# Splitting the attention values in half-length buffers, at other steps around the turn of a head, with low parts made by a negated copy and an adding transfer

## The chip, the cores and the metric

One Trainium2 chip, one core. The metric is the time of one execution in device microseconds; lower is better. The times given are medians of several executions, and the profile is of one of them.

## The reference

One inference step of a decoder layer, for a prompt of 1024 positions and 8 sampled sequences of one position each, in float32. Only the first part of it, the differential attention of the prompt, is touched:

```python
def diff_attention(q, k, v, q_pos, k_pos, rel_bias, lam):
    ...
    def probs(qi, ki):
        s = jnp.einsum('bqhd,bkhd->bhqk', qi, ki).astype(f32) * scale + bias
        return jax.nn.softmax(jnp.where(mask, s, neg), axis=-1)

    attn = probs(q1, k1) - lam * probs(q2, k2)
    return jnp.einsum('bhqk,bkhd->bqhd', attn, v.astype(f32))

def reference(...):
    ...
        hp = rmsnorm(xp, norm_mix[l])
        qa, ka, va, qr, kr, vr, gr = project(hp, w_in[l])
        oa = diff_attention_prompt(qa, ka, va, rel_bias, lam)
        s_p, o_r = retention_prompt(...)
        xp = xp + merge_groups(oa, o_r, gr, subln_a[l], lam_init) @ w_out[l]
        xp = xp + mem_attend(rmsnorm(xp, norm_mem_q[l]), mk_p, mv_p, w_mq[l], w_mo[l])
        xp = xp + sq_relu_mlp(rmsnorm(xp, norm_mlp[l]), w_up[l], w_down[l])
    ... the same for the 8 sampled sequences, with a paged cache of 256 positions
```

There are 4 attention heads with values of width 128; `attn` is causal, so a block of 128 queries meets only the blocks of 128 keys up to its own.

## The kernel before, in words

**Exact products from fast ones.** The matrix engine works on `float32r`, a shorter float. Each operand is split in a high part (a copy that rounds to `float32r`) and a low part (the operand less its high part), and a product is three matmuls: high by high, high by low, low by high.

**The attention of the prompt** goes head by head. A head has ten items `(pr, kg)`: query pair `pr` (256 queries, 0 to 3) by key pair `kg` (256 keys, 0 to `pr`), in the order (0,0), (1,0), (1,1), (2,0), (2,1), (2,2), (3,0), (3,1), (3,2), (3,3). The loop `for g in range(-4, 40)` has one step per item; `h` is the head and `x` the item's number, 0 to 9, and `g` from -4 to -1 is a run-up (`h` = -1, `x` = 6 to 9). One step

- turns the probabilities of the next item (`turn`, `trA`): 3 or 4 transposes on TensorE, a rounding copy `ah` on ScalarE (L1034), the low part `al` on VectorE (L1035); for the item on the diagonal GpSimd clears a quarter of both (L1033);
- computes scores of later query blocks (`scores`, the list `SCORES`; steps 6 to 9 those of the next head): matmuls `sp` in one of 3 banks of PSUM, the masked minimum `mn` and the result `e` on VectorE (L1001), an exponential on ScalarE (L1007), and, after the second of the two maps, the weighted difference on VectorE (L1014 to L1016);
- weighs the values with the item (`weigh`, `av`): for each of two key blocks the three matmuls by `VH` and `VL`; an item with key pair `kg` reads the key blocks `2 * kg` and `2 * kg + 1`. After the last key pair of a query pair ScalarE copies the sum (L1053);
- fills the rest with matmuls of the next heads' query and key projection (`filler`, `qkp`), and in head 3 with the sampled sequences' decode (`dsc`).

**The values.** `fetch_values(h + 1)`, at step `x == VALUES_AT` (6), has SyncE's queue bring the next head's values from HBM into `vraw`, 512 KB, in a buffer of a ring of three (`raw`) that the weights, the broadcast row factors `rbh` and the decode's gathered keys `ck` share. `load_values(h)`, at `x == 0`, makes `VH` and `VL`, each one buffer of 1024 columns: for each half a copy on ScalarE (L975) and a subtraction on GpSimd, in one case on VectorE (L977). Key blocks 0 to 3 (`kg` 0 and 1) lie in the first half, blocks 4 to 7 (`kg` 2 and 3) in the second. So the first half is last read at step 7 of a head, and the second is first read at step 5 and last at step 9.

**What sets the order.** Every engine takes its instructions in one order, and so does each DMA queue (SyncE's and GpSimd's). Matmuls of this part keep the order of the program (`pin`). On the other engines the framework orders the instructions itself when the kernel is built, from their place in the program and its own estimates of when they can start; `tc.issue_after` puts some behind a named instruction. So an instruction can stand earlier than its step: the decode's gathers are written at steps 21 to 26 and are issued by GpSimd from 341.80 us on, in head 1.

Beside these, `load_part` (L949 to L958) prepares the next head's keys and queries, with transfers on GpSimd's queue (L950, L952), `norm_out` (L1119) scales the head before by `rbh`, and `operand_steps` (L1255) loads the output projection's operands, 2064 KB each, on GpSimd's queue.

Of the kernel before, what the change touches and what calls it, by code (L numbers as in the profile page):

```python
# [10 lines left out]
F32 = mybir.dt.float32  # L11
F32R = mybir.dt.float32r
I32 = mybir.dt.int32
AF = mybir.ActivationFunctionType
ALU = mybir.AluOpType
# [4 lines left out]
P = 128  # L20
D = 1024
NT = 1024
# [26 lines left out]
def decoder_step(ctx: ExitStack, tc: tile.TileContext, i: dict, o: dict):  # L49
    nc = tc.nc  # L50
# [47 lines left out]
    half = G.tile([P, 1], F32, tag="half", name="half")  # L98
# [86 lines left out]
    V = v_front.enter_context(pool("v"))  # L185
# [95 lines left out]
    with pool("s") as A:  # L281
# [64 lines left out]
        for t in range(9):  # L346
# [13 lines left out]
            if t in (1, 3, 5):  # L360
                k = t // 2 + 1
# [24 lines left out]
    with pool("a") as A:  # L386
# [56 lines left out]
        with behind("Activation", "DVE"):  # L443
# [3 lines left out]
            for k in range(4):  # L447
                src = t2f[k // 2][:, k % 2, :]
# [189 lines left out]
        A = r_front.enter_context(pool("r", side="right"))  # L638
# [245 lines left out]
    with pool("b") as A:  # L884
# [13 lines left out]
        def head_units(h):  # L898
            uqk[h] = [unit(U_QK + 2 * h + x) for x in range(2)]
# [61 lines left out]
        vraws = {}  # L961

        def fetch_values(h):
            vraw = vraws[h] = G.tile([P, 1024], F32, tag="raw", name=f"vraw_{h}", bufs=3)
            nc.sync.dma_start(
                vraw[:, :NT].rearrange("p (t v) -> p t v", t=8),
                o["v_p"][:, h * P : h * P + P].rearrange("(t p) v -> p t v", p=P),
            )

        def load_values(h):  # L970
            VH = A.tile([P, NT], F32R, tag="VH", name=f"VH_{h}")
            VL = A.tile([P, NT], F32R, tag="VL", name=f"VL_{h}")
            vraw = vraws[h]
            for cs in (slice(0, 512), slice(512, NT)):
                nc.scalar.copy(VH[:, cs], vraw[:, cs])  # L975
                eng = nc.vector if h == 3 and cs.start == 0 else nc.gpsimd
                eng.tensor_sub(VL[:, cs], vraw[:, cs], VH[:, cs].bitcast(F32))  # L977
            vals[h] = VH, VL
            oraws[h] = A.tile([P, NT], F32, tag="oraw", name=f"oraw_{h}", bufs=2)

        def scores(h, q, m):
            KA, KB, Q, M = stacks[h]
# [54 lines left out]

        def weigh(h, pr, kg):
            ah, al = trs.pop((h, pr, kg))
            VH, VL = vals[h]  # L1040
            nk = 2 * pr + 2
            if kg == 0:
                avs[h, pr] = PS.tile([P, 512], F32, tag="av", name=f"av_{h}_{pr}", bufs=1)
            av = avs[h, pr]
            for kk in range(2):
                k = 2 * kg + kk
                at_ = (1 - kk if kg == pr else kk) * 256
                ks, xs = slice(k * P, k * P + P), slice(at_, at_ + 256)
                mm(av[:, :256], VH[:, ks], ah[:, xs], k == 0, False)
                mm(av[:, :256], VH[:, ks], al[:, xs], False, False)  # L1050
                mm(av[:, :256], VL[:, ks], ah[:, xs], False, k == nk - 1)
            if k == nk - 1:
                nc.scalar.copy(oraws[h][:, pr * 256 : pr * 256 + 256], av[:, :256])  # L1053
# [275 lines left out]
        for g in range(-4, 40):  # L1329
            h, x = divmod(g, 10)  # L1330
            todo = []
            if g >= 0:
                if x == 0:
                    load_values(h)
                    if h < 2:
                        head_units(h + 2)
            if h < 3:
                if h >= 0 and x == EARLY_AT[0]:
                    load_stacks(h + 1)
                    until(h + 1, 1, 1)  # L1340
                    early = load_part(h + 1, EARLY)
                for y in (0, 1, 2, 3):
                    if h >= 0 and x == EARLY_AT[y]:
                        if y == 2:
                            until(h + 1, 1, 0)
                        next(early)
                if x == LATE_AT[0]:
                    until(h + 1, 2, 1)
                    late = load_part(h + 1, LATE)
                for y in (0, 1, 2, 3):  # L1350
                    if x == LATE_AT[y]:
                        if y == 2:
                            until(h + 1, 2, 0)
                        next(late)
            if x == VALUES_AT and h < 3:
                fetch_values(h + 1)
            if g in DECODE_AT:
                next(decode)
            if 0 <= g + 1 < 40:
                todo.append(lambda: turn(*items[g + 1]))  # L1360
            for q, m in SCORES.get(x, ()):
                hh = h + (x >= 5)
                if hh < 4:
                    todo.append(lambda q=q, m=m, hh=hh: scores(hh, q, m))
            if g >= 0:
                todo.insert(2, lambda: weigh(*items[g]))
            if h > 0:
                at_ = NORM_AT[h == 3]
                if x == at_[0]:
                    todo.append(lambda: sqs.append(norm_sums(h - 1)))  # L1370
                if x == at_[1]:
                    todo.append(lambda: sqs.append(norm_factors(h - 1, sqs.pop())))
                if x == at_[2]:
                    todo.append(lambda: sqs.append(norm_send(h - 1, sqs.pop())))
                if x == at_[3]:
                    todo.append(lambda: norm_row(h - 1, sqs.pop()))
                if x == at_[4]:
                    with tc.issue_after(seen["DVE"]):
                        norm_out(h - 1)
            dec = (3, 2, 0) in done  # L1380
            n = DFILL[g - 28] if dec else FILL - (g > 17)
            for y, f in enumerate(todo):
                f()
                for _ in range(shares(y + 1, n, len(todo), dec) - shares(y, n, len(todo), dec)):

                    if dec or (3, 2, 0) not in done:
                        next(filler, None)
            for _ in range(OPERAND_AT.count(g)):
                next(par)
            if g in OUT_AT:  # L1390
                for _ in range(OUT_AT[g]):
                    next(ahead, None)
            if g == LOADS_AT:

                for x, nm in enumerate(("KA0", "KA1", "KB0", "KB1")):
                    raw = A.tile([P, NT], F32R, tag=nm, name=f"raw_o{x}").bitcast(F32)
                    nc.sync.dma_start(raw, i["wall"][U_OUT + x])
                    raws_out.append(raw)
                onesb.append(A.tile([P, NT], F32, tag="M", name="onesb")[:, :P])
                nc.gpsimd.memset(onesb[0], 1.0)  # L1400
            if g in UNITS_AT:
                x = len(us_out)
                with tc.issue_after(seen["ACT"]), tc.issue_after(seen["E"]):
                    us_out.append(unit(U_OUT + x, raw=raws_out[x]))
# [3 lines left out]
        while len(us_out) < 4:  # L1408
            x = len(us_out)
# [1028 lines left out]
}  # L2438
EARLY_AT, LATE_AT = (3, 4, 4, 5), (7, 7, 8, 8)
NORM_AT = (2, 3, 4, 5, 8), (2, 5, 6, 8, 9)  # L2440
VALUES_AT = 6
DECODE_AT = (21, 22, 25, 26)
OPERAND_AT = (30, 30, 30, 33, 33, 34)
LOADS_AT, UNITS_AT = 32, (34, 35, 37, 38)
# [182 lines left out]
```

## Time and profile before

| | |
|---|---|
| median of 3 runs | 1493.73 us (1493.14 to 1497.79) |
| the profiled execution's span, first to last instruction | 1492.5 us |
| TensorE matmuls busy | 1474.0 us, 99% |
| VectorE, ScalarE, GpSimd busy | 1102.5, 678.4, 325.4 us |
| granted TensorE clock | 0.998 |
| the attention's value matmuls (`av`) | 271.6 to 442.5 us of the span |

The profiled execution's own time is its span and the little that lies around it; the median is 1.2 us above the span. In a row of a timeline stand the start and the duration in us, the engine, the line, the operation, what it writes and reads, and in brackets how long the engine had been idle before and what ended that. PE is TensorE, ACT ScalarE, DVE VectorE, POOL GpSimd, SPq the queue of SyncE. Each engine's row in the table is a busy time: what it is worth to shorten one depends on who waits for it.

### The profile page before, as it was taken

The numbers are of one execution on the slowest core, as the hardware profiler recorded it, in microseconds if no ns is written. First come the engines' busy times: TensorE is split into PE (matmuls) and PEld (weight loads), VectorE is DVE, ScalarE is ACT, GpSimd is POOL, SyncE is SP. The second block draws the span as 40 slices with busy tenths as digits, with TensorE's granted clock in tenths as the row PEclk, the third lists the DMA queues.
The fourth block names the chain that finished last, engine by engine and source line by source line (L and its number), as shares of the span: only waits on it lengthen the run. The fifth ranks groups of instructions, "written<-read, shape, count | busy, mean of one in ns | idle before, by whom it ended". The sixth has DMA issues, their size and how long they took to land.

```text
span 1492.5 us, 27826 instructions
## 1 busy us (share of the span) xinstructions
PE 1474.0 (99%) x10893; PEld 1402.5 (94%) x10893; DVE 1102.5 (74%) x2279; ACT 678.4 (45%) x1326; POOL 325.4 (22%) x346
## 2 busy tenths in 40 slices
PE   9999999998999999999999999999999999999997
PEld 7899779998769999989999999999999999999997
DVE  7656636987877734567786978888888889787875
ACT  7534435665652432147535634334344444343454
POOL 0035323114414321104132000000001311020380
PEclk9999999999999999999999999999999999999999
DMA  8155737214857157483592443344436674536273
GB/s 292 61 186 168 201 71 181 80 34 123 232 181 279 49 191 193 132 238 103 165 321 72 128 149 137 141 156 157 142 141 210 237 265 142 172 99 191 81 129 114
DMA packets 125229, 236.67 MB, mean 159 GB/s; under 512 B 13744, under 2 KB 76517, under 8 KB 124970
## 3 DMA queue, kind: packets, MB, share of 16 engines
q1 hardware_dynamic: 89056, 170.50, 36.5%
q0 software_dynamic: 24912, 44.80, 10.9%
q10 hardware_dynamic: 11130, 19.60, 3.5%
q8 instruction: 85, 1.39, 0.4%
q14 instruction: 46, 0.38, 0.1%
HBM read 170.24 MB, written 57.52 MB: 153 GB/s over the span
## 4 chain that ended last, share of the span: by engine, by line
PE 90%; DVE 5%; ACT 2%; issue 1%; DMA 1%; ACTq 0%; POOL 0%; DVEq 0%; SPq 0%
PE dn L2309 21%; PE Z L2143 9%; PE qkp L75 7%; PE pr_o L75 6%; PE mq L75 6%; PE pr_m L75 6%; PE X L2143 6%; PE Y L2143 6%; PE grp L75 3%; PE sp L75 2%; PE av L75 2%; PE mv L75 2%; PE mk L75 1%; PE mpv L75 1%; PE vap_z L522 1%
## 5 line engine op out<-in xcount | busy, mean ns | idle before, releaser
L2309 PE MATMUL dn<-UH,wd 128*128 128x258 f32 x1792 | 324.6, 283 | 0.0
L2309 PEld LDWEIGHTS dn<-UH,wd 128*128 128x128 f32 x1792 | 277.5, 189 | 0.7 <-ACT c L2410 0.2
L2309 PE MATMUL dn<-UL,wd 128*128 128x258 f32 x896 | 252.8, 282 | 0.0
L2309 PEld LDWEIGHTS dn<-UL,wd 128*128 128x128 f32 x896 | 169.0, 189 | 0.0
L2413 DVE TENSOR_TENSOR c<-c,dn 128x258 f32<-128x258 f32 x216 | 88.9, 418 | 38.5 <-PE dn L2309 36.1
L2169 ACT ACTIVATE hq<-r 128x258 f32<-128x258 f32 x128 | 53.7, 421 | 118.3 <-DVE r L2168 118.3
L2143 PE MATMUL Z<-T_h,wu 128*128 128x258 f32 x512 | 98.2, 284 | 0.0
L2143 PE MATMUL X<-UH,wu 128*128 128x258 f32 x512 | 97.4, 282 | 0.0
L2287 ACT CAST wd<-raw_d 128x512 fp32r<-128x512 f32 x96 | 58.8, 620 | 79.0 <-PE dn L2309 74.6
L1953 ACT CAST wu<-raw_up 128x512 fp32r<-128x512 f32 x96 | 59.1, 617 | 59.9 <-PE Z L2143 50.0
L2280 ACT CAST UH<-raw_h 128x1032 fp32r<-128x1032 f32 x56 | 58.7, 1056 | 53.5 <-PE dn L2309 27.7
L2143 PEld LDWEIGHTS X<-UH,wu 128*128 128x128 f32 x512 | 81.3, 188 | 0.2 <-ACT p L2194 0.2
L2143 PEld LDWEIGHTS Z<-T_h,wu 128*128 128x128 f32 x512 | 81.3, 189 | 0.0
L2180 POOL DMA_DIRECT2D HT<-ht x32 | 17.2, 538 | 292.3 <-DVE ht L2179 291.8
L2281 DVE TENSOR_TENSOR UL<-raw_h,UH 128x1032 fp32r<-128x1032 f32 x56 | 73.6, 1315 | 8.6 <-ACT UH L2280 8.6
L2288 DVE TENSOR_TENSOR wd<-raw_d,wd 128x512 fp32r<-128x512 f32 x96 | 72.2, 759 | 10.0 <-ACT wd L2287 9.9
L2143 PE MATMUL Z<-T_l,wu 128*128 128x258 f32 x256 | 72.3, 282 | 0.0
L2143 PE MATMUL X<-UL,wu 128*128 128x258 f32 x256 | 72.3, 282 | 0.0
L128 ACT CAST wh_u<-raw_u 128x1024 fp32r<-128x1024 f32 x43 | 44.6, 1047 | 54.3 <-PE mq L75 31.1
L1954 DVE TENSOR_TENSOR wu<-raw_up,wu 128x512 fp32r<-128x512 f32 x96 | 64.7, 687 | 3.5 <-ACT wu L1953 3.5
L2301 POOL TENSOR_TENSOR raw_d<-raw_d,raw_d 128x512 f32<-128x512 f32 x16 | 22.1, 1383 | 193.8 <-DVE raw_d L2297 172.9
L129 DVE TENSOR_TENSOR wl_u<-raw_u,wh_u 128x1024 fp32r<-128x1024 f32 x39 | 49.4, 1273 | 18.8 <-ACT wh_u L128 18.6
(597 smaller groups left out, 4732.8 us busy)
## 6 DMA issues: line engine op xcount, KB each, us to landing
raw_u<-in_wall SPq DMA_DIRECT2D x49, 512.0 KB
HT<-ht POOLq DMA_DIRECT2D x32, 516.0 KB
raw_h<-HT SPq DMA_DIRECT2D x32, 516.0 KB
raw_up<-in_wall SPq DMA_DIRECT2D x32, 512.0 KB
raw_d<-in_wall SPq DMA_DIRECT2D x32, 512.0 KB
HQ<-hq ACTq DMA_DIRECT2D x32, 387.0 KB
raw_h<-HQ SPq DMA_DIRECT2D x24, 516.0 KB
cmk<-in_cmk SPq DMA_DIRECT2D x16, 512.0 KB
```

The costliest lines, as they stand in the source:

```text
L75: pinned(nc.tensor.matmul(out, l, r, start=start, stop=stop))
L129: (lo_engine or nc.vector).tensor_sub(wl[:, :n], raw[:, :n], wh[:, :n].bitcast(F32))
L1953: nc.scalar.copy(w[:, :512], src)
L1954: nc.vector.tensor_sub(w[:, 512:], src, w[:, :512].bitcast(F32))
L2143: pinned(nc.tensor.matmul(ps, l, r[:, k, :], start=first and k == 0 and x == 0, stop=k == 3 and x == 2, skip_group_check=True))
L2169: nc.scalar.activation(h[:, PLACE[quad], :], r, AF.Square)
L2280: nc.scalar.copy(h, rv)
L2281: nc.vector.tensor_sub(l, rv, h.bitcast(F32))
L2287: nc.scalar.copy(w[:, :512], src)
L2288: nc.vector.tensor_sub(w[:, 512:], src, w[:, :512].bitcast(F32))
L2309: pinned(nc.tensor.matmul(ps, l, r[:, k, cq], start=first and k == 0 and x == 0, stop=k == 3 and x == 2, skip_group_check=True))
L2413: nc.vector.tensor_add(y, y, ps)
```

## The change

The values of a head get four buffers of 512 columns, `VH0`, `VL0`, `VH1`, `VL1`, in the place of two of 1024. The first half of the next head is split at step 8 of the head before it (two steps after the fetch), the second half at step 2 of its own head. The low part is no longer a subtraction: ScalarE writes the negated high part into it, and a transfer on GpSimd's queue adds the raw values to it. `weigh` reads the half that its key pair lies in. The tile that collects a head's result (`oraws`) is named at the first `weigh` in the place of `load_values`.

```diff
-        def load_values(h):
-            VH = A.tile([P, NT], F32R, tag="VH", name=f"VH_{h}")
-            VL = A.tile([P, NT], F32R, tag="VL", name=f"VL_{h}")
-            vraw = vraws[h]
-            for cs in (slice(0, 512), slice(512, NT)):
-                nc.scalar.copy(VH[:, cs], vraw[:, cs])
-                eng = nc.vector if h == 3 and cs.start == 0 else nc.gpsimd
-                eng.tensor_sub(VL[:, cs], vraw[:, cs], VH[:, cs].bitcast(F32))
-            vals[h] = VH, VL
-            oraws[h] = A.tile([P, NT], F32, tag="oraw", name=f"oraw_{h}", bufs=2)
+        def load_values(h, half):
+            vh, vl = (A.tile([P, 512], F32R, tag=f"V{x}{half}", name=f"V{x}{half}_{h}") for x in "HL")
+            src = vraws[h][:, 512 * half : 512 * half + 512]
+            nc.scalar.copy(vh, src)
+            nc.scalar.activation(vl, vh.bitcast(F32), AF.Copy, scale=-1.0)
+            nc.gpsimd.dma_start(vl, src, accum_op=ALU.add)
+            vals[h, half] = vh, vl
...
         def weigh(h, pr, kg):
             ah, al = trs.pop((h, pr, kg))
-            VH, VL = vals[h]
+            VH, VL = vals[h, kg // 2]
             nk = 2 * pr + 2
+            if (pr, kg) == (0, 0):
+                oraws[h] = A.tile([P, NT], F32, tag="oraw", name=f"oraw_{h}", bufs=2)
...
-                ks, xs = slice(k * P, k * P + P), slice(at_, at_ + 256)
+                ks, xs = slice(k % 4 * P, k % 4 * P + P), slice(at_, at_ + 256)
...
-                if x == 0:
-                    load_values(h)
-                    if h < 2:
-                        head_units(h + 2)
+                if x == 0 and h < 2:
+                    head_units(h + 2)
+                if x == VALUES_AT[2]:
+                    load_values(h, 1)
...
-            if x == VALUES_AT and h < 3:
+            if x == VALUES_AT[0] and h < 3:
                 fetch_values(h + 1)
+            if x == VALUES_AT[1] and h < 3:
+                load_values(h + 1, 0)
...
-VALUES_AT = 6
+VALUES_AT = 6, 8, 2
```

## The prediction, made before the change was run

> **What bounds the kernel now.** I read the page's head and its chain first, then the matrix engine's own waits and busy time in the attention part (235 to 445 us of the span), then the instruction timeline at the three turns of a head.
>
> ```profile
> span 1492.5 us, 27826 instructions
> PE 1474.0 (99%) x10893; PEld 1402.5 (94%) x10893; DVE 1102.5 (74%) x2279; ACT 678.4 (45%) x1326; POOL 325.4 (22%) x346
> ...
> PE 90%; DVE 5%; ACT 2%; issue 1%; DMA 1%; ACTq 0%; POOL 0%; DVEq 0%; SPq 0%
> ```
>
> TensorE is the bound: 1492.5 - 1474.0 = 18.5 us of it are idle in the whole span, and that is all that a change which touches no matmul can win. The waits of TensorE in the attention part, then its idle moments at the turns 1 to 2 and 2 to 3:
>
> ```profile
> PE sp L75 <- DVE mn L1001: 3.9, 4, 1.6
> PE trA L78 <- DVE e L1016: 2.6, 3, 2.0
> PE hrT L78 <- DVE c L1068: 0.3, 1, 0.3
> ...
> 352.12 0.41 PE L75 MATMUL sp<-KA,Q 128*128 128x320 f32 x1 [0.64 <-DVE mn L1001]
> 354.28 0.42 PE L75 MATMUL sp<-KA,Q 128*128 128x320 f32 x1 [1.60 <-DVE mn L1001]
> 359.87 0.55 PE L78 MATMUL trA<-ident,e 128*128 128x128 f32 x3 [2.03 <-DVE e L1016]
> 399.24 0.41 PE L75 MATMUL sp<-KA,Q 128*128 128x320 f32 x1 [0.82 <-DVE mn L1001]
> ```
>
> So 3.9 + 2.6 + 0.3 = 6.8 us are idle there (the columns of the first three lines: total, times, longest), all put down to VectorE, none to the values: no row says that a matmul waits for VH or VL. 0.64 + 1.60 + 2.03 = 4.3 us lie at the turn from head 1 to 2. In the stretch of the turn 0 to 1 TensorE is never idle, though the same reload is done there (columns: stretch, its length, busy time of TensorE's matmuls and weight loads, VectorE, ScalarE, GpSimd, then the granted clock, the DMA engines' share and GB/s):
>
> ```profile
> 300.00:310.00 10.00, 10.00 (x70) 9.79 (x69) 9.61 (x32) 6.32 (x20) 0.77 (x4) 1.00 0.00 0
> ```
>
> What the reload does to VectorE at the turn 1 to 2 is seen here:
>
> ```profile
> 355.25 0.21 DVE L1015 SCALAR_TENSOR_TENSOR mn<-mn,nlam,sm 128x1 f32<-128x1 f32 x1
> 356.76 2.50 POOL L977 TENSOR_TENSOR VL<-vraw,VH 128x512 fp32r<-128x512 f32 x2 [2.95 <-ACT VH L975]
> 356.84 1.22 DVE L1015 SCALAR_TENSOR_TENSOR mn<-mn,nlam,sm 128x1 f32<-128x1 f32 x1
> 358.45 1.37 DVE L1016 SCALAR_TENSOR_TENSOR e<-e,mn,e 128x512 f32<-128x512 f32 x1
> 403.50 0.75 DVE L1016 SCALAR_TENSOR_TENSOR e<-e,mn,e 128x512 f32<-128x512 f32 x1
> ```
>
> While the two subtractions run on GpSimd (356.76 to 359.26), one VectorE instruction takes 1.22 instead of 0.21 us, and one takes 1.37 instead of 0.75. The second ends at 359.82, and the transposes that wait for it start at 359.87.
>
> **The change, part by part.**
>
> *Low parts no longer subtracted.* These are the instructions that go, and the nearest row for what comes:
>
> ```profile
> L975 ACT CAST VH<-vraw x8: 615/622/625, 244.8 to 403.0; 128x512 fp32r<-128x512 f32 x8
> L977 POOL TENSOR_TENSOR VL<-vraw,VH x7: 1254/1287/1640, 245.5 to 403.7; 128x512 fp32r<-128x512 f32 x7
> L977 DVE TENSOR_TENSOR VL<-vraw,VH x1: 693/693/693, 402.9 to 402.9; 128x512 fp32r<-128x512 f32 x1
> 1424.48 17.95 POOL L2417 DMA_DIRECT2D c<-c  x20
> ```
>
> GpSimd loses 7 x 1.29 = 9 us and gains 8 issues of an adding transfer. The adding transfers at the end of the kernel take 17.95 / 20 = 0.90 us of it each: 7 us. Neither is on TensorE's path. What is, is the collision above: without it the two VectorE instructions end (1.22 - 0.21) + (1.37 - 0.75) = 1.6 us earlier. I take -1.5 us, since the 2.03 us wait bounds it at -2.0 and about half a microsecond of it then remains: late next is the same VectorE row, by its own queue. The other end is 0, if an issue of a transfer holds VectorE as a subtraction does. The one subtraction on VectorE, 0.69 us at 402.9, comes after the wait at 399.24 and I take 0 for it: the decode's matmuls, which fill head 3, cover it; without that cover it would be worth 0.69.
>
> *ScalarE's negated copies.* 8 x 0.62 = 5.0 us more (the row of VH; the copy of VL has that shape). In the window of 215 us ScalarE is busy 124.87, so it has 90 us of idle time, and the nearest gaps are these:
>
> ```profile
> 305.64 0.62 ACT L1007 ACTIVATE e<-e,mn 128x384 f32<-128x384 f32 x1 [2.10 <-DVE mn L1001]
> 350.53 0.48 ACT L1034 CAST ah<-trA 128x384 fp32r<-128x384 f32 x1 [2.38 <-PE sp L75]
> 394.18 0.51 ACT L1007 ACTIVATE e<-e,mn 128x256 f32<-128x256 f32 x1 [1.37 <-DVE e L1016]
> ...
> sum 215.00, PE 208.00 PEld 184.22 DVE 171.05 ACT 124.87 POOL 63.37; mean PE 11.56 PEld 10.23 DVE 9.50 ACT 6.94 POOL 3.52
> ```
>
> A pair of copies is 1.24 us, and each of the three gaps holds one. I count 0; 5.0 us is the ceiling if no gap were met. The second half, at step 2, waits for nothing (its buffer is free from the last matmul of the head before) and the gaps there are about 1 us: 0 as well.
>
> *Half buffers, filled from step 8 on.* The wait of the first copy for the last matmul of the old head goes; since no matmul waited for VH, that is worth 0. New is what the copies can wait for: the fetch of the raw values, still issued at step 6.
>
> ```profile
> 240.73 0.38 SPq L965 DMA_DIRECT2D vraw<-out_v_p  x1
> 340.89 0.49 SPq L965 DMA_DIRECT2D vraw<-out_v_p  x1
> 388.50 0.70 SPq L965 DMA_DIRECT2D vraw<-out_v_p  x1
> ...
> 244.76 1.14 ACT L975 CAST VH<-vraw 128x512 fp32r<-128x512 f32 x2 [1.83 <-DMA vraw<-out_v_p]
> ...
> 343.49 0.28 PE L75 MATMUL av<-ah,VH 128*128 128x256 f32 x1
> 392.24 0.28 PE L75 MATMUL av<-ah,VH 128*128 128x256 f32 x1
> ...
> 345.00:350.00 5.00, 5.00 (x34) 4.86 (x33) 3.79 (x12) 2.25 (x7) 3.92 (x7) 1.00 1.13 317
> 390.00:395.00 5.00, 5.00 (x39) 4.95 (x38) 3.34 (x15) 2.52 (x9) 4.16 (x7) 1.00 1.09 236
> ```
>
> The first fetch had landed 4.0 us after its issue, when the copy started that had waited 1.83 us for it. By that pace the fetches of heads 2 and 3 land at 344.9 and 392.5, just as the step 7 matmuls (343.49 and 392.24, the last readers of the half) are done. But the DMA engines are full there (shares 1.13 and 1.09), with the broadcast of a row, as large as the fetch and just ahead of it on SyncE's queue, and the decode gathers in the same stretch: twice 512 KB at half of the two rows' mean, 277 GB/s, is 7.5 us, so my estimate is 348.4 and 396. A ScalarE that stands at the copy holds up the exponentials queued behind it; VectorE waits for those, TensorE for VectorE. The floor is 0 (the gap before 350.53 takes it); the ceiling is 4 us at each turn (348.4 - 344.4, 396 - 393, and a pair of copies). As the order of ScalarE's queue is the framework's, I cannot read it; I take 0.5 us for both, near the floor, because the gap of 2.38 us stands just where the estimate falls.
>
> *The adding transfer's landing.* It must be there for the third matmul of the new head:
>
> ```profile
> 161.23 0.85 POOL L675 DMA_DIRECT2D OPH<-rh  x1 [1.06 <-ACT rh L672]
> 171.13 0.59 ACT L672 CAST rh<-trR 128x512 fp32r<-128x512 f32 x1 [3.66 <-DMA OPH<-rh]
> ...
> 362.13 0.28 PE L75 MATMUL av<-ah,VL 128*128 128x256 f32 x1
> 394.23 0.87 POOL L1255 DMA_DIRECT2D UL<-OPL  x1
> 407.60 0.27 PE L75 MATMUL av<-ah,VL 128*128 128x256 f32 x1
> ```
>
> The nearest transfer of 256 KB from GpSimd's queue, on full DMA engines, is known to be done 171.13 - 161.23 = 9.9 us after its issue. With copies done at 349.6 and 397.3 and that latency, VL lands at 359.5 and 407.2, before 362.13 - 1.5 = 360.6 and at 407.6: nothing, with no margin at the second. So 0 is taken, and 3 us is the other end, when GpSimd's in-order queue (the eight gathers, or the 2064 KB load at 394.23) is in front. The Trainium skill, "DMA: Bandwidth & Descriptors", section "Anatomy of one DMA — SWDGE (gpsimd) path", gives about 2.0 us fixed plus the bytes over 436 GB/s, by which an estimate for 256 KB is 2.6 us; the landing would then have 7 us to spare and this rival would be dead. The row of this trace does not agree, since it shows up to 9.9 us under load, and I go by the row.
>
> The buffer of the raw values is freed one half later. The next user of the last one is a pair of decode gathers:
>
> ```profile
> 409.19 1.00 POOL L859 DMA_INDIRECT ck<-in_cache_kT,idk  x1 [0.51 <-POOL al L1033]
> 427.58 1.07 PE L75 MATMUL dsc<-ck,qblkd 128*64 128x512 f32 x2
> ```
>
> 18 us lie between their issue and their matmul, and step 2 of head 3 is two steps of 4.5 us behind its step 0 (407.60 - 362.13 for ten), so it costs 0; if they land late, what is late next is that matmul, 1 us at most.
>
> **Sum:** -1.5 + 0 + 0 + 0.5 + 0 = -1.0 us against the profiled execution's span of 1492.5, thus 1491.5. The median of the runs shown, 1493.73, is 1.2 above that span: 1492.7 us. The difference from no change that a measurement of this kernel can tell is 0.3%, 4.5 us (1489.2 to 1498.2): I forecast no change.
>
> **Rivals.**
>
> *Slower: ScalarE stands at the fetch.* Place: the queue of ScalarE at steps 7 and 8 of heads 1 and 2. If the copies stand ahead of the exponentials there (394.18 above; the one of that shape at head 1 starts at 345.83, below), ScalarE waits from about 344 to 348 and from 393 to 396 or later.
>
> ```profile
> 345.83 0.51 ACT L1007 ACTIVATE e<-e,mn 128x256 f32<-128x256 f32 x1
> ```
>
> Price: 2 to 3 us on TensorE at each turn where part of a gap covers it, 4 where none does. Without the 0.5 us of the sum the forecast is 1492.2; one turn gives 1492.2 + 2.5 = 1494.7, both at their ceiling 1492.2 + 8 = 1500.2. It decides when the fetch lands more than 2.4 us after the copy's place in the queue; slower by 0.3% takes 6 us of it. For it: the rows of full DMA engines and the one copy that has already waited 1.83 us. Against: the gap of 2.38 us.
>
> *Cancelled: the transfer lands late.* TensorE then waits at the first value matmul for VL, 3 us at the turns 1 to 2 and 2 to 3 together: 1492.2 + 3 = 1495.2. For it the 9.9 us, against it the pace of the first fetch, 512 KB in 4.0 us.
>
> *Faster: VectorE's other waits go too.* The waits of 0.64, 1.60 and 0.82 us come from VectorE working off the low part of the last turned block ahead of the masks of (2,1) and (3,0). With ScalarE's order at step 8 new, these may swap as they stand at the turn 0 to 1, where TensorE has no wait. With the 2.03 that is 5.1 us: 1493.73 - 5.1 = 1488.6; the floor is all 6.8 us, 1486.9. Against it: no part of the change touches these instructions.
>
> **How the numbers follow.** The small gain (1490.5 to 1494.5) has 0.52; ScalarE at the fetch 0.28, of which 0.15 lies beyond 1498.2; the late landing 0.08; the faster rival 0.12. So faster 0.12, same 0.52 + 0.13 + 0.08 = 0.73, slower 0.15. The range for 8 in 10 runs from 1488.6, which leaves out half of the faster case (0.06), to 1499.0, which leaves out the worst of the first rival (0.11).
>
> **What would show it.** No GpSimd subtraction and no VectorE row of 1.2 us for a 128x1 at the turn 1 to 2; the wait of 2.03 us down to about 0.5; eight issues of about 0.9 us on GpSimd; ScalarE's first copies at steps 8 with no wait on the fetch. Wrong would be the forecast if ScalarE's waits on the fetch sum to over 3 us, if a value matmul waits for a DMA, or if TensorE's idle time in the attention part is under 3 or over 10 us.

## The result, and the profile after

The change made the kernel slower: 1503.04 us (median; 1501.62 to 1503.74) beside 1494.24 us of the kernel before on the same chip, a ratio of 1.0052, interval 1.0041 to 1.0062. Measured a second time, with other kernels beside it, the ratio was 1.0039 (1.0025 to 1.0053). The forecast was no change, with 1499.0 us as the upper end of its range.

The head of the page of the changed kernel, whose profiled execution took 1501.62 us:

```profile
span 1499.8 us, 27839 instructions
PE 1478.1 (99%) x10893; PEld 1405.3 (94%) x10893; DVE 1099.9 (73%) x2278; ACT 682.3 (45%) x1334; POOL 318.6 (21%) x347
```

The span grew by 7.3 us. TensorE is idle for 21.7 us instead of 18.5, and it is also busy for 4.1 us more, with the same 10893 matmuls. So part of the loss is a slower TensorE, not a waiting one.

To place the 7.3 us, I took from each trace the first score matmul (line 75, `sp`) and the first value matmul (`av<-ah,VH`) of each head; in the kernel before these stand at 255.31, then 271.56, 313.29, 361.90 and 407.25, and the last `av<-ah,VH` at 442.28. The distances between the starts of these matmuls, in us, for all kernels that were run:

| kernel | first score to head 0 | head 0 to 1 | 1 to 2 | 2 to 3 | 3 to last value matmul | ratio to before |
|---|---|---|---|---|---|---|
| before | 16.25 | 41.73 | 48.61 | 45.35 | 35.03 | 1 |
| before, second profile | 16.24 | 41.73 | 48.13 | 45.40 | 35.04 | 1 |
| changed | 18.56 | 41.73 | 49.02 | 49.90 | 35.04 | 1.0052 |
| changed, second profile | 19.74 | 41.69 | 49.22 | 50.81 | 35.04 | 1.0039 |
| changed, fetch at step 4 | 17.53 | 41.73 | 43.87 | 45.05 | 35.54 | 1.0017 |
| the same, second profile | 17.21 | 41.72 | 45.39 | 45.05 | 35.57 | 0.9996 |
| changed, head 0 subtracted | 16.24 | 41.73 | 46.50 | 50.45 | 35.03 | 1.0055 |
| both of these edits | 16.53 | 41.73 | 45.36 | 45.08 | 35.40 | **0.9977** |
| changed, copy behind (2,0) | 19.25 | 41.71 | 46.94 | 45.81 | 36.40 | 1.0008 |
| changed, copies written at the turn | 18.37 | 41.73 | 49.52 | 49.88 | 35.03 | 1.0040 |
| half buffers, subtraction | 16.24 | 42.78 | 49.08 | 49.42 | 35.04 | 1.0070 |
| the same, fetch at step 4 | 16.24 | 42.78 | 47.95 | 46.93 | 35.06 | 0.9990 |
| before, new low parts | 18.89 | 41.71 | 45.11 | 47.23 | 46.13 | 1.0096 |
| before, fetch at step 4 | 16.26 | 41.73 | 47.92 | 45.38 | 35.03 | 1.0000 |

Before against changed: 2.3 us are lost ahead of the first value matmul, 0.4 at the turn 1 to 2, 4.55 at the turn 2 to 3. That is 7.3 us, as much as the span grew. What lies ahead of the first score matmul is 0.6 us shorter and what lies behind the last value matmul 0.6 us longer, which cancels.

Each ratio compares a kernel with the kernel before on the same chip, but the chips differ. On the one where the first runs of "fetch at step 4", "head 0 subtracted", "half buffers, subtraction" and "before, new low parts" were made, the kernel before took 1490.64 us at a granted clock of 0.998 in most executions; on two others it took 1494.92 and 1495.62 us at 0.996. The one changed kernel that was run on both sorts, with the fetch at step 4, has 1.0017 on the first and 0.9996 on another. So ratios from different chips can differ by 0.2%; why the chips differ is not shown.

**The turns.** Timelines of the changed kernel: the fetch on SyncE's queue, ScalarE's first copy of the half, then what VectorE and TensorE wait for; first at the turn 1 to 2, then at 2 to 3 (start, length, engine and line; in brackets the idle time ahead of it and what ended it).

```profile
341.27 1.18 SPq L965 DMA_DIRECT2D vraw<-out_v_p  x1
351.08 0.62 ACT L973 CAST VH<-vraw 128x512 fp32r<-128x512 f32 x1 [5.31 <-PE av L75]
352.08 0.50 ACT L1004 ACTIVATE e<-e,mn 128x256 f32<-128x256 f32 x1
352.21 0.50 DVE L958 TENSOR_TENSOR Q<-qraw,Q 64x336 fp32r<-64x336 f32 x1 [4.01 <-ACT Q L957]
355.01 0.44 PE L78 MATMUL trA<-ident,e 128*128 128x128 f32 x2 [2.48 <-issue]
356.55 0.42 PE L75 MATMUL sp<-KA,Q 128*128 128x320 f32 x1 [0.63 <-DVE mn L998]
...
390.70 0.70 SPq L965 DMA_DIRECT2D vraw<-out_v_p  x1
398.92 0.62 ACT L973 CAST VH<-vraw 128x512 fp32r<-128x512 f32 x1 [3.92 <-PE sp L75]
399.45 0.50 ACT L1004 ACTIVATE e<-e,mn 128x256 f32<-128x256 f32 x1
402.35 0.69 PE L78 MATMUL trA<-ident,e 128*128 128x128 f32 x2 [3.39 <-DVE e L1013]
```

ScalarE stands still for 5.31 and 3.92 us ahead of the copy. The profile names a matmul as releaser, but the last `av` of the old half had ended at about 345.9, five microseconds earlier: the copy waited for the fetch, which was there 9.8 us after its issue (8.2 us at the other turn). Behind the copy in ScalarE's queue stands the exponential of block (1,1), 128x256; it starts at 352.08, while in the kernel before it started at 345.83 (that head began 1.75 us earlier there). VectorE waits for ScalarE, TensorE for VectorE.

The clock shows the second half of the loss (columns: stretch, its length, TensorE's busy time and matmuls, granted clock, DMA share, GB/s):

```profile
352.00:356.00 4.00, 1.44 (x9) 1.00 0.85 300
356.00:360.00 4.00, 3.40 (x14) 0.66 0.72 197
360.00:364.00 4.00, 4.00 (x26) 0.92 0.27 47
...
398.00:402.00 4.00, 0.96 (x5) 0.95 1.14 333
402.00:406.00 4.00, 3.54 (x8) 0.50 1.17 407
406.00:410.00 4.00, 4.00 (x12) 0.69 1.06 343
410.00:414.00 4.00, 4.00 (x18) 1.00 1.12 422
```

After the idle time the granted clock is at half for a while. (1 - 0.66) x 4 + (1 - 0.92) x 4 = 1.7 us of full-speed work are lost at the first turn, up to 0.2 + 2.0 + 1.24 = 3.4 at the second.

**The gain that was forecast.** At the turn 1 to 2 the pair of VectorE instructions that was stretched to 1.22 and 1.37 us beside GpSimd's subtractions now reads:

```profile
359.72 0.21 DVE L1012 SCALAR_TENSOR_TENSOR mn<-mn,nlam,sm 128x1 f32<-128x1 f32 x1
360.32 0.74 DVE L1013 SCALAR_TENSOR_TENSOR e<-e,mn,e 128x512 f32<-128x512 f32 x1
```

and the 2.03 us wait for them is gone. TensorE's waits at this turn go from 4.3 to 3.1 us and the clock takes 1.7, which together gives the 0.4 us or so by which the turn is longer. Whether the new low parts are what took the 2.03 us away is not shown by this profile: the second profile of the kernel before, below, does not have that wait either.

**Ahead of head 0.** The issue of the second pair of weight blocks, ScalarE's cast of them and TensorE's waits, first in the kernel before, then in the changed one:

```profile
248.03 3.83 SPq L122 DMA_DIRECT2D raw_u<-in_wall  x2
256.13 1.05 ACT L128 CAST wh_u<-raw_u 128x1024 fp32r<-128x1024 f32 x1
268.15 0.41 PE L75 MATMUL sp<-KA,Q 128*128 128x320 f32 x1 [0.86 <-DVE mn L1001]
```

```profile
251.43 1.25 SPq L122 DMA_DIRECT2D raw_u<-in_wall  x2
257.88 1.05 ACT L128 CAST wh_u<-raw_u 128x1024 fp32r<-128x1024 f32 x1 [2.35 <-PE sp L75]
260.59 0.44 PE L75 MATMUL sp<-KA,Q 128*128 128x384 f32 x1 [1.11 <-DVE mn L998]
269.89 0.42 PE L75 MATMUL sp<-KA,Q 128*128 128x320 f32 x1 [1.76 <-DVE mn L998]
```

and the wait of SyncE's queue ahead of this issue in the changed kernel (total, times, longest; before, it was 3.3 us for the subtraction on GpSimd):

```profile
SPq L122 <- DMA VL<-vraw: 11.0, 1, 11.0
```

The weights' fetch `raw_u` takes the buffer (tag "raw") that held head 0's raw values. It is free when the low parts have been made. A subtraction on GpSimd ends soon after its copy; the adding transfer has first to be issued, one after the other half's, and then to land. SyncE waits 11.0 us, the fetch goes out 3.4 us later, ScalarE's cast waits 2.35 us for it with the exponentials behind it, and TensorE idles 1.11 and 1.76 us where it had 0.86.

### The profile page after: what moved, and what is told of

It reads as the page before. It is cut to its first block, busy times and chain, and to the rows that moved or that the text cites. A ratio compares the mean times of both kernels' runs of the same rounds, so it can differ in the third digit from the quotient of the medians.

```text
span 1499.8 us, 27839 instructions
## 1 busy us (share of the span) xinstructions
PE 1478.1 (99%) x10893; PEld 1405.3 (94%) x10893; DVE 1099.9 (73%) x2278; ACT 682.3 (45%) x1334; POOL 318.6 (21%) x347
## 3 DMA queue, kind: packets, MB, share of 16 engines
q0 software_dynamic: 26064, 46.90, 11.7%
## 4 chain that ended last, share of the span: by engine, by line
PE 66%; DVE 3%; DMA 1%; ACT 1%; issue 1%; DVEq 0%; ACTq 0%
PE dn L2310 19%; PE Z L2144 9%; PE pr_o L75 6%; PE mq L75 6%; PE pr_m L75 6%; PE X L2144 6%; PE Y L2144 6%; PE mv L75 1%; PE mk L75 1%; PE mpv L75 1%; PE dsc L75 1%; PE ms L75 1%; DMA raw_h<-HQ 1%; DMA raw_h<-HT 1%; DVE UL L2282 1%
```

## Experiments

The theories: **A**, ScalarE stands at the fetch at two turns, and the clock halves behind it; **D**, the raw buffer is freed late ahead of head 0. Rivals: **B**, the new low parts cost in themselves; **C**, an earlier fetch only moves the wait; **H**, an early fetch would make any of these kernels faster; and, for single runs, those named there.

### The fetch two steps earlier

```
-            if x == VALUES_AT[0] and h < 3:
+            if g in (-4, 4, 14, 24):
                 fetch_values(h + 1)
```

> The changed kernel with one edit: the raw values of heads 1 to 3 are fetched two steps earlier (step 4 of the head before instead of step 6). Theory A (ScalarE stands at the fetch at the turns 1 to 2 and 2 to 3, TensorE then idles and its granted clock halves): the waits of 5.31 and 3.92 us ahead of ScalarE's copies go, the clock stays at 1.00 from 350 to 410, and the 0.4 + 4.55 us that these two turns cost go, some more with the lock of VectorE no longer there: 1503.0 - 5.0 to 6.5 = 1496.5 to 1498.0; the first value matmul of head 0 stays at about 273.3. Rival B (the adding transfers or the extra copies cost in themselves): at most 1 us is gained, 1502 to 1503. Rival C (an earlier fetch pushes the broadcast rows and gathers back): the wait only changes its name, 1501 to 1505.

Measured: ratio 1.0017 (1.0008 to 1.0027), where the changed kernel had 1.0052. The profiled execution is the fastest of eleven. The copies' rows, then all waits of TensorE from 235 to 452 us (total, times, longest):

```profile
345.67 0.62 ACT L973 CAST VH<-vraw 128x512 fp32r<-128x512 f32 x1 [0.23 <-PE av L75]
389.71 0.62 ACT L973 CAST VH<-vraw 128x512 fp32r<-128x512 f32 x1 [0.22 <-PE av L75]
```

```profile
PE sp L75 <- DVE mn L998: 2.6, 2, 1.8
PE trA L78 <- DVE e L1013: 0.6, 2, 0.4
PE hrT L78 <- DVE c L1067: 0.3, 1, 0.3
PE av L75 <- DMA VL<-vraw: 0.2, 1, 0.2
```

ScalarE no longer waits, the clock is 1.00 in all stretches from 350 to 420, and the two turns are 5.15 and 4.85 us shorter than in the changed kernel: theory A holds, C falls. The distance to head 0 still has 1.3 us too much, with the 1.75 us wait ahead of it. The turn 1 to 2 is 4.7 us shorter than in the kernel *before*: with the fetch out of the way TensorE does not wait for VectorE there at all in this profile.

The same kernel again, with another profile:

> The kernel with the fetch at step 4 a second time, beside the three others of this call. Its times lay between 1490.7 and 1496.3 us, and only the fastest was profiled. Theory G (the wait of 1.75 us ahead of the first value matmuls halves the clock in some executions and not in others, as it did with 1.76 and 1.79 us in two other kernels): the spread is there again, some 4 us and more from end to end; if the profiled execution is one of the slow ones, it shows the clock at 0.5 to 0.7 between 270 and 274. The ratio is 1.000 to 1.003. Rival (the adding transfer lands late in the slow ones): a value matmul waits 1 us or more for VL.

Ratio 0.9996 (0.9986 to 1.0007), times from 1492.1 to 1498.4: the spread is there again, and the profiled execution, 1496.27 us, lies in its upper part. But theory G does not explain it: the clock is 1.00 at 270. It halved somewhere else, in the middle of dense work; this is the stretch in the second profile (in the first it has 36 matmuls at 1.00):

```profile
786.00:790.00 4.00, 4.00 (x23) 0.59 0.01 1
```

It also had one wait of 1.7 us late in the kernel and 1.5 us more at the turn 1 to 2. The value matmuls waited 0.3 us, so the rival falls too. The second profile of the kernel before shows such a halving there as well (clock 0.90 in 780 to 790). The two ratios of this kernel, 1.0017 and 0.9996, come from two chips and their intervals do not overlap: it lies between level with the kernel before and 0.2% slower, both times below the changed kernel's 1.0039 and 1.0052.

### The kernel before with an early fetch

```
-            if x == VALUES_AT and h < 3:
+            if g in (-4, 4, 14, 24):
                 fetch_values(h + 1)
```

> The kernel before with nothing but the fetches at step 4: the control for the early fetch. Theory A: in the kernel before nothing waits for the fetch of heads 2 and 3, so the early fetch gives nothing: ratio 0.999 to 1.001, and the waits of 0.64, 1.60 and 2.03 us (or 2.44 in one piece) stay at the turn 1 to 2. Rival H (the early fetch makes the turn faster whatever the values' buffers are): the turn 1 to 2 is 4 us shorter here too, ratio 0.996 to 0.998, and the gain of the kernel with both edits has nothing to do with the change.

Ratio 1.0000 (0.9991 to 1.0009); the turn 1 to 2 takes 47.92 us, with one wait of 2.43 us. A VectorE instruction is stretched here too (1.74 us for the 128x512 of line 1016, beside the subtraction at 357.85), but no matmul is shown waiting for it. Rival H falls: in the kernel before nothing waits for the fetch, and its place is worth nothing. It became a cost only with the half buffers.

### The fetch late, the copy behind the exponentials

```
             if x == VALUES_AT[1] and h < 3:
-                load_values(h + 1, 0)
+                with tc.issue_after(seen["ACT"]) if h >= 0 else nullcontext():
+                    load_values(h + 1, 0)
```

> The changed kernel, the fetch still at step 6, but ScalarE's copy of the first half is put behind the exponential of block (2,0) in ScalarE's queue instead of ahead of that of (1,1). Theory A in its narrow form (not the late fetch costs, but what is queued behind the copy that waits for it): the exponentials of (1,1) and (2,0) start at about 347 and 395 as in the kernel before although the copy still waits until 351 and 399; TensorE idles less than 2 us in a piece, the clock stays at 1.00, and 7 to 10 us go: ratio 0.999 to 1.001. Rival F (the values are needed so early that the late fetch costs in any place): TensorE waits for VH or VL at the first value matmuls, ratio 1.003 to 1.006.

Ratio 1.0008 (0.9999 to 1.0017). The fetch lands as late as before, the copies start at about the same times as in the changed kernel:

```profile
350.09 0.62 ACT L1004 ACTIVATE e<-e,mn 128x384 f32<-128x384 f32 x1
351.79 0.62 ACT L973 CAST VH<-vraw 128x512 fp32r<-128x512 f32 x1 [0.99 <-issue]
...
398.76 0.62 ACT L973 CAST VH<-vraw 128x512 fp32r<-128x512 f32 x1 [0.78 <-DMA vraw<-out_v_p]
...
410.76 0.39 PE L75 MATMUL av<-ah,VL 128*128 128x256 f32 x1 [1.07 <-DMA VL<-vraw]
```

but the exponentials of (1,1) and (2,0) are through by then, and the turns are 2.1 and 4.1 us shorter than in the changed kernel. So it was not the late landing that cost most, but what stood in the queue behind the instruction that waited for it. What TensorE still waits is 2.30 us in one piece at the turn 1 to 2, where less than 2 had been expected, 1.93 us at 400.83 for ScalarE's copy `qblkd`, which stands behind the copies of the values here, and 1.07 us at a value matmul of head 3 for VL, whose transfer is issued 8.6 us ahead of the head's first value matmul here and 11.4 in the changed kernel. The clock stays at 1.00 at both turns. The gain on the changed kernel, 0.3 to 0.4%, is less than the 7 to 10 us that had been expected. Rival F, by which the late fetch costs in any place and the ratio is 1.003 to 1.006, falls, though the wait for VL is a part of it.

### The step at which the copy is written

```
-            if x == VALUES_AT[1] and h < 3:
-                load_values(h + 1, 0)
...
+                if x == 0:
+                    load_values(h, 0)
```

> The changed kernel with the copies of the first half written at step 0 of their own head instead of step 8 of the head before; the half buffers, the adding transfers and the fetch at step 6 stay. Theory I (the free half buffer, not the step at which the copy is written, lets it move ahead in ScalarE's queue): the copy still stands ahead of the exponential of (1,1), ScalarE waits for the fetch as in the changed kernel, ratio 1.003 to 1.007. Rival (the step decides): the copy comes after the turn, no wait for the fetch, 0.998 to 1.001, or a wait for VL at the first value matmuls as in the kernel with the method at the old steps, 1.008 or more.

Ratio 1.0040 (1.0027 to 1.0053), as the changed kernel on the same chip (1.0039). The copy waits for the fetch just as long: 5.54 us ahead of 350.54 and 3.89 us ahead of 398.57, each time in front of the exponential of (1,1).

The step 8 in the program decides nothing. Once the half buffer is free early, the framework sets the copy ahead of the exponential of (1,1) by itself.

### Half buffers without the new low parts

```
-            nc.scalar.activation(vl, vh.bitcast(F32), AF.Copy, scale=-1.0)
-            nc.gpsimd.dma_start(vl, src, accum_op=ALU.add)
+            eng = nc.vector if h == 3 and half == 0 else nc.gpsimd
+            eng.tensor_sub(vl, src, vh.bitcast(F32))
```

> The changed kernel with the low parts by subtraction as in the kernel before (GpSimd, and VectorE for the first half of head 3): the half buffers and their steps alone. Theory A (the fetch is what the turns cost) with theory D (the 2.3 us ahead of the first value matmul come from the raw buffer that the adding transfer frees late): the two waits of ScalarE stay, the first value matmul of head 0 is back at about 271.6, so 1503.0 - 2.3 = 1500.7, up to 1502.5 if the subtractions meet VectorE again. Rival B (the low parts' new method is what costs): back to the time of before, 1494 to 1495.

Ratio 1.0070 (1.0057 to 1.0084), somewhat above what theory A gave (1500.7 to 1502.5 on 1494.2, so 1.0044 to 1.0056); it was measured on the chip on which the kernel before is faster. The distance to head 0 is 16.24 us again, as D says; the two stalls stay:

```profile
351.00 0.62 ACT L973 CAST VH<-vraw 128x512 fp32r<-128x512 f32 x1 [4.78 <-DMA vraw<-out_v_p]
398.58 0.62 ACT L973 CAST VH<-vraw 128x512 fp32r<-128x512 f32 x1 [3.58 <-DMA vraw<-out_v_p]
```

Here the profile names the fetch itself as releaser. Rival B falls as the cause of the loss: it is there without any adding transfer.

The same with the fetch at step 4:

> Half buffers with the low parts by subtraction (as in the run of the subtraction) and the fetch at step 4: no adding transfer, no ScalarE wait for the fetch. Theory A: the run of the subtraction stood at 1.0070 with two stalls of TensorE at halved clock, which cost 5 us each there or more; both go: ratio 0.999 to 1.002. VectorE can still meet GpSimd's subtractions at the turn 1 to 2, worth up to 2 us. Rival B (it is the half buffers or the new steps as such that cost): 1.004 or more.

Ratio 0.9990 (0.9981 to 0.9999). The subtractions meet VectorE again (one 128x1 of line 1012 takes 1.25 us at 357.84, beside GpSimd's subtraction at 357.80), and TensorE waits 1.24 and 1.47 us at the turn 1 to 2.

### The new low parts in the old buffers

```
-                eng = nc.vector if h == 3 and cs.start == 0 else nc.gpsimd
-                eng.tensor_sub(VL[:, cs], vraw[:, cs], VH[:, cs].bitcast(F32))
+                nc.scalar.activation(VL[:, cs], VH[:, cs].bitcast(F32), AF.Copy, scale=-1.0)
+                nc.gpsimd.dma_start(VL[:, cs], vraw[:, cs], accum_op=ALU.add)
```

> The kernel before with only the low parts changed: ScalarE's negated copy and an adding transfer, in the full-length buffers and at the old steps. Theory D (late release of head 0's raw values) without A: the first value matmul of head 0 comes 1.8 to 2.3 us later, the wait of 2.03 us at the turn 1 to 2 shrinks to about 0.5, ScalarE does not wait for a fetch: 1494.2 + 2.3 - 1.5 = 1495.0, within 1493.5 and 1497. Rival B (the method costs in itself): 1499 to 1503, with value matmuls that wait for VL after the turns, since here the transfer starts only after the last value matmul of the old head.

Ratio 1.0096 (1.0081 to 1.0112), the slowest of all. Value matmuls wait for VL, worst in head 3 (two issues on GpSimd, then the matmul):

```profile
402.83 0.82 POOL L1255 DMA_DIRECT2D UH<-OPH  x1
406.12 0.95 POOL L977 DMA_DIRECT2D VL<-vraw  x1 [2.47 <-ACT VL L976]
417.79 0.58 PE L75 MATMUL av<-ah,VL 128*128 128x256 f32 x1 [8.17 <-DMA VL<-vraw]
```

The transfer is there 11.7 us after its issue. The forecast by theory D, 1493.5 to 1497 us, was far off: the median is 1505.78 us, beyond rival B's 1503 too. This is the pattern of rival B, though only in these buffers, and it says what the half buffers are for: the transfer must start before the turn, and in full-length buffers it can't. Ahead of it on GpSimd's queue stands a load of 2064 KB (first row). With the fetch at step 4 the adding transfer also stood behind such a load, issued at 390.81, and landed 12.7 us after its own issue at 391.61, against a median of 4.7 us for that kernel's eight. How much of this the queue ahead costs, and how much the full DMA engines, was not tried. The lost run-up of theory D is there too (18.89 us).

### Head 0 by subtraction

```
+            if h == 0:
+                nc.gpsimd.tensor_sub(vl, src, vh.bitcast(F32))
+            else:
                 nc.scalar.activation(vl, vh.bitcast(F32), AF.Copy, scale=-1.0)
                 nc.gpsimd.dma_start(vl, src, accum_op=ALU.add)
```

> The changed kernel with head 0's low parts alone by GpSimd's subtraction; heads 1 to 3 keep the adding transfer. Theory D: the raw buffer is free as early as before, the weights of head 2 are fetched at about 248 instead of 251.4, ScalarE's cast of them does not wait, the first value matmul of head 0 stands at about 271.5 instead of 273.3: 1503.0 - 2.3 = 1500.7. Rival E (the run-up is late because of ScalarE's two extra copies or a different order of the work, not the buffer): 1502.5 to 1503.5. The turns are as in the changed kernel by both.

In the trace theory D holds exactly: the weights' fetch is issued at 247.50, ScalarE's cast does not wait, the distance to head 0 is 16.24 us instead of 18.56. The ratio does not show it: 1.0055 (1.0042 to 1.0069), where about 1.004 follows from 2.3 us less. The distance 2 to 3 is 0.5 us longer than in the changed kernel, 1 to 2 is 2.5 us shorter (ScalarE waits 3.69 us for the fetch there instead of 5.31, and the clock stays at 1.00), though by both theories the turns were to be as in the changed kernel. The profiled execution is the fastest of five, and the chip is the one on which the kernel before is faster; the changed kernel itself was not run there. So from this run alone the worth of D in time stays open.

Together with the early fetch it can be seen:

> The changed kernel with both edits: fetches of heads 1 to 3 at step 4, and head 0's low parts by GpSimd's subtraction. Theories A and D together: with the fetch at step 4 alone the ratio to the kernel before was 1.0017 and the wait of 1.75 us ahead of the first value matmuls stayed; now the weights' fetch is issued at 248 instead of 252, that wait is 0.85 as before, and 1.3 to 2.3 us go: ratio 1.0001 to 1.0008. By the profiles alone (span 1488.9 with the fetch at step 4, less the run-up) it would be 1487 and a ratio of 0.997. Rival (the remaining 0.17% is the adding transfer that lands just in time, 0.25 us of wait at the first value matmul of head 3, and later in other executions): 1.001 to 1.002, unchanged.

Ratio 0.9977 (0.9968 to 0.9987): faster than the kernel before by 3.4 us, and better than the forecast of 1.0001 to 1.0008. That forecast started from 1.0017, measured on another chip; from 0.9996 the same 1.3 to 2.3 us give 0.9981 to 0.9987. This is the best kernel of the study; it was measured once, on one chip. The waits of TensorE from 235 to 452 us:

```profile
PE sp L75 <- DVE mn L1001: 1.4, 2, 0.8
PE trA L78 <- DVE e L1016: 1.0, 3, 0.4
PE sp L75 <- DVE al L1035: 0.6, 1, 0.6
PE hrT L78 <- DVE c L1070: 0.3, 1, 0.3
PE sp L75 <- DMA KB<-KB: 0.2, 1, 0.2
```

These are 3.5 us instead of 6.8 in the kernel before, and the distances sum to 2.9 us less.

### Both kernels again

> The kernel before once more, for a profile on the same chip as these runs. If chips differ in nothing but a constant, its waits at the turn 1 to 2 are 0.64, 1.60 and 2.03 us as in the first profile, with the clock at 1.00. If the waits vary from execution to execution, at least one of them is different by over 0.5 us.

> The changed kernel a second time, as the measure for the others on this chip. Theory A: ScalarE again waits 4 us and more ahead of the copies of heads 2 and 3 and TensorE 2.5 us or more at both turns, ratio 1.004 to 1.007. If the first profile was an unlucky one: waits under 2 us at one of the two turns.

The kernel before has other waits in its second profile: one of 2.44 us at the turn 1 to 2 instead of 0.64, 1.60 and 2.03. Behind it the clock halves, which it did not in the first profile; in the first profile the 4 us after the wait of 2.03 us stay at 1.00 (second fence):

```profile
350.00:354.00 4.00, 1.56 (x11) 1.00 0.91 295
354.00:358.00 4.00, 3.95 (x17) 0.57 0.20 72
```

```profile
356.00:360.00 4.00, 1.97 (x14) 1.00 0.00 0
360.00:364.00 4.00, 4.00 (x28) 1.00 0.02 6
```

The turn takes 48.13 and 48.61 us. The 2.03 us wait is missing in the second profile, and so is the stretched pair of VectorE rows, though the two subtractions are there:

```profile
357.46 0.74 DVE L1016 SCALAR_TENSOR_TENSOR e<-e,mn,e 128x512 f32<-128x512 f32 x1
357.65 2.96 POOL L977 TENSOR_TENSOR VL<-vraw,VH 128x512 fp32r<-128x512 f32 x2 [4.12 <-ACT VH L975]
```

Here VectorE's instruction starts first and keeps its 0.74 us, and it is GpSimd that takes longer (2.96 instead of 2.50 us for the two subtractions). So the wait on which the forecast gain rests comes and goes with the timing of the kernel before.

The changed kernel has its two stalls again, ScalarE's waits are 4.57 and 4.69 us, put down to the fetch by name; the first profile was not an unlucky one. TensorE waits 4.15 us at the turn 2 to 3, but 1.74 us in one piece at the turn 1 to 2, less than the 2.5 expected; the clock halves behind both.

## Why the prediction was wrong

- **Low parts off GpSimd, -1.5 us: not seen in the changed kernel, and shown in part with the early fetch.** The collision is gone, but one of two profiles of the kernel before has none either, and the half buffers with subtraction are no slower at the turns (49.08 and 49.42 us) than the changed kernel (49.02 and 49.90): where ScalarE stalls, no gain is seen. With the early fetch the turn 1 to 2 takes 47.95 us by subtraction, with one stretched row and a wait of 1.47 us behind it, and 43.87 to 45.39 with the new low parts. Between the two of these kernels that differ only in the low parts of heads 1 to 3, the ratio goes from 0.9990 to 0.9977, about 2 us; the intervals overlap a little, so this size is uncertain. That it came out near 1.5 is in part luck, as the wait that it was read from is not always there.
- **ScalarE's negated copies, 0: right.** The best kernel has six of them, and its waits are half of those before.
- **ScalarE at the fetch, 0.5 us: this is the step that failed.** It measured 3.6 to 5.2 us at the turn 1 to 2 (49.02 against 45.39 and 43.87) and 4.85 at the turn 2 to 3 (49.90 against 45.05). It failed in three places. The landing was put at 348.4 and 396 and came at 351 and 399. The queue was called unreadable, and then the kinder order was taken: the gap of 2.38 us covers the wait only if the copy stands in that gap, and it stood two exponentials ahead of it. And idle time was priced as idle time, so that 4 us was called a ceiling; with the halved clock the turn 2 to 3 lost 4.85. The first rival had the right place and mechanism, with 0.28; its condition ("more than 2.4 us after the copy's place") was met, with 5.3 and 3.9 us; its price of 8 us for both turns was close, and the 1500.2 us that it came to lacks only what the raw buffer cost.
- **The adding transfer's landing, 0 with 3 as the other end: right for the changed kernel**, where no value matmul waited. The row of 9.9 us was the right measure of it: under the load of the turn 2 to 3, behind a load of 2064 KB, it took 11.7 us in the old buffers and 12.7 in the half buffers with the early fetch. By the Trainium skill, "DMA: Bandwidth & Descriptors", section "Anatomy of one DMA — SWDGE (gpsimd) path", the estimate was 2.6 us; the traces don't agree under load.
- **The raw buffer freed later, 0: this failed too, by 2.3 us.** The text looked at the next user of the last raw buffer and found 18 us of room. The next user of the first one, head 0's, is a weights' fetch on SyncE's queue, with ScalarE's cast and the exponentials behind it, and there was no room at all.
- **The faster rival** was right about what could be had: with the fetch early and the new low parts, the waits for VectorE at the turn 1 to 2 do shrink, to 1.0 us and less. The early fetch alone (47.92 us), or with half buffers and subtraction (47.95), does not do it; why the rest of the waits goes was not tried. In the changed kernel the stall took their place.

Of what would show it: the eight issues on GpSimd, the missing long VectorE row and the missing 2.03 us wait came as said; the last two are no proof, since a profile of the kernel before has them as well. The sum of ScalarE's waits on the fetch (9.2 us against a limit of 3) and TensorE's idle time (10.1 us against 10) say that it was wrong.

## What to carry to other kernels

A buffer that comes free earlier lets a scheduler move the producer (the instruction that fills it) ahead, and the producer then waits for *its* input at the head of an in-order queue: when a buffer wait is taken away, move the load ahead by as much, and ask what stands behind the instruction that waits. When a consumer is made slower or asynchronous, follow every use of the source buffer to its next owner, the first and not only the last. And price a stall of a busy TensorE at more than its length, since the clock may halve behind it.

## What the runs showed of the hardware

The granted clock can halve after idle times shorter than I had thought, and not each time. The changed kernel idles just ahead of 270 for 1.76 us in its first profile and 1.79 in its second; here is what follows in each:

```profile
270.00:274.00 4.00, 4.00 (x28) 1.00 0.31 117
```

```profile
270.00:274.00 4.00, 3.99 (x19) 0.68 0.36 123
274.00:278.00 4.00, 4.00 (x27) 0.89 0.00 0
```

A wait of 2.30 us (copy behind, at 357) and one of 2.03 us (before) left the clock at 1.00, one of 2.44 us (before, second profile) did not; and at 786 it halved behind 0.26 us of idle time and a group of very narrow matmuls. No threshold can be read from these. The half-speed time is much the same each time where the wait was short: here (0.32 + 0.11) x 4 = 1.7 us are lost, that is 3.4 us at half, and in the kernel before 0.43 x 4, the same.

The Trainium skill, "TensorE: Matmul & The Clock Gate", "Part 1: The HAM clock gate (the "warmup" mystery)", tells of a free-running window of about 3.4 us, half clock after an idle one and full clock after a busy one. The 3.4 us agree, and a free-running window would explain that the same wait halves the clock in one execution and not in another; but that a whole window must be idle doesn't agree with 1.79 us. What share of a window decides was not tried.

How long VectorE's rows last beside GpSimd's subtractions depends on which of the two starts first. A row that starts while a subtraction is already running is stretched: from 0.21 to 1.22 us and from 0.75 to 1.37 (before), from 0.21 to 1.25 (half buffers, subtraction, fetch at step 4), from 0.74 to 1.74 (before, fetch at step 4). A row that starts 0.2 us ahead of it keeps its 0.74 us (before, second profile). This is read from the few rows of the weighted difference (128x1 and 128x512) at the turn 1 to 2; the masks `e<-sp,M` of VectorE in the same stretch keep their length.
